# Label-smoothed cross entropy: a ring of three 8000-column buffers, the shorter transfers into buffers of their own, wide tiles worked in two pieces

## The chip, the core and the metric

The kernel runs on one core of a Trainium2 chip. Five engines matter here: PE (TensorE, matrix products), DVE (VectorE, elementwise work and reductions), ACT (ScalarE, functions such as exp and ln), POOL (GpSimd) and SP (SyncE), which computes nothing and here issues the transfers from the chip's main memory into the core's own memory (SBUF). The metric is device time in microseconds (us), from launch to the end of the program.

## The reference

There are 256 rows of 32000 float32 logits and one label to a row. For every row the kernel owes one number:

```python
log_probs = logits - max(logits); log_probs -= log(sum(exp(log_probs)))
smooth_targets[:] = smoothing / num_classes
smooth_targets[i, label] = 1.0 - smoothing + smoothing / num_classes
out = -sum(smooth_targets * log_probs)
```

Since the targets of a row sum to one, the result is log(sum(exp(x))) minus a weighted sum of the logits, in which all have the small weight and the label's logit has the large one besides. So each logit has to be read once (32.77 MB in all), and goes into two sums: one of the logits, one of their exponentials. The kernel takes exp without subtracting the maximum.

## The kernel before, in words

Each of the 128 partitions holds two rows of the input, one after the other, as one line of 64000 columns. The columns are cut into 14 transfers by the table `WIDTHS` (L17): three of 10672, 10672 and 10656 for the first row of each partition, eleven of 8224, 6032, 4480, 3392, 2576, 1984, 1552, 1216, 992, 832 and 720 for the second. A transfer brings one piece of each of the 128 lines; one column of all partitions is 512 bytes.

`load` (L154) issues a transfer on SP (L159). Widths of 1600 and over (`RING_MIN`) go into a ring of three buffers, `xt`, each as wide as the widest tile. That is the first nine transfers, so that the fourth to the ninth wait until the tile three places earlier has been read by DVE and ACT. The five narrower ones go into buffers of their own, `xl`, and wait for no reader. But SP issues in the order of the program, so they stand behind the ninth transfer.

There is one more rule, which the framework adds: transfers of SP and ACT share eight completion semaphores in turn, and a transfer isn't issued before the one that had its semaphore last has landed. The small transfer of the labels, issued by ACT (L103), takes the second of the eight.

Every tile gets two instructions. `sum_logits` (L162) is one pass of DVE that adds the left half of the tile to the right half and accumulates the sum; its elementwise output `jd` is scratch. `sum_exps` (L175) is one pass of ACT that takes exp and accumulates; its elementwise output is scratch too. For tiles wider than 2576 columns (`TURN_MAX`) it goes into the one buffer `ja`, and each such pass waits for the pass before it; the narrower ones take turns in three buffers `jt`. On both engines a short instruction follows that reads the accumulator.

POOL computes the address of each label's logit, fetches these logits with two indirect transfers, and scales them into column 0 of `xsum`. At the end of a row `finish` (L182) takes the logarithm on ACT (L186, L188), turns the two columns of 128 numbers into rows on PE (L190, L194), and combines them on DVE (L195). For the second row the last tiles' sums are added up stepwise (L247 to L255), so that little is left after the last tile; SP then writes the result (L259).

Of the kernel before, what the change touches and what calls it, by code (L numbers as in the profile page):

```python
# [8 lines left out]
FP32 = mybir.dt.float32  # L9
BF16 = mybir.dt.bfloat16  # L10
I32 = mybir.dt.int32
ALU = mybir.AluOpType
AF = mybir.ActivationFunctionType
AX = mybir.AxisListType


WIDTHS = (  # L17
    (10672, 10672, 10656),
    (8224, 6032, 4480, 3392, 2576, 1984, 1552, 1216, 992, 832, 720),
)  # L20

RING_MIN = 1600

TURN_MAX = 2576


def _exp_ln_table(arch: str) -> int | None:
# [30 lines left out]
def kernel(  # L58
# [7 lines left out]
    nc = tc.nc  # L66
    nc.at_finalize(_issue_first_transfers_at_start)
    B, C = logits.shape
    P = nc.NUM_PARTITIONS
# [10 lines left out]
    junk = ctx.enter_context(tc.tile_pool(name="junk", bufs=1))  # L80
    turn = ctx.enter_context(tc.tile_pool(name="turn", bufs=3))
# [7 lines left out]
    if tbl is not None:  # L89
        nc.scalar.add_instruction(  # L90
            mybir.InstLoadActFuncSet(
                name=nc.get_next_instruction_name(),
# [11 lines left out]
        out=lab[:], in_=labels.bitcast(I32).rearrange("(p f) -> p f", p=P)  # L104
    )
    rowoff = small.tile([P, R], I32, name="rowoff", tag="rowoff")
    for r in range(R):
        nc.gpsimd.iota(
            out=rowoff[:, r : r + 1],
# [6 lines left out]
        out=flat_idx[:],  # L116
        in0=rowoff[:],
        in1=lab[:].rearrange("p (r two) -> p r two", two=2)[:, :, 0:1],
        op=ALU.add,
    )  # L120
    gat = small.tile([P, R], FP32, name="gat", tag="gat")
    for r in range(R):
        nc.gpsimd.indirect_dma_start(  # L123
            out=gat[:, r : r + 1],
            out_offset=None,
            in_=logits[:],
# [4 lines left out]
    make_identity(nc, ident[:])  # L131

    label_weight = c_big / c_small
    xsums, esums = [], []
    for r in range(R):
        n = len(WIDTHS[r])
        xsum = small.tile([P, n + 1], FP32, name=f"xsum{r}", tag=f"xsum{r}")  # L140
        esum = small.tile([P, n], FP32, name=f"esum{r}", tag=f"esum{r}")
        nc.gpsimd.tensor_scalar(  # L142
            out=xsum[:, 0:1],
            in0=gat[:, r : r + 1],
            scalar1=label_weight,
            scalar2=None,
            op0=ALU.mult,
        )
        xsums.append(xsum)
        esums.append(esum)  # L150
# [3 lines left out]
    def load(w: int, col: int, name: str):  # L154
        if w >= RING_MIN:
            xt = ring.tile([P, max(WIDTHS[0])], FP32, name="xt", tag="xt")
        else:
            xt = tail.tile([P, w], FP32, name=name, tag=name)
        nc.sync.dma_start(out=xt[:, :w], in_=x[:, col : col + w])  # L159
        return xt  # L160

    def sum_logits(xt, w: int, out: bass.AP):  # L162
        h = w // 2
        jd = junk.tile([P, max(WIDTHS[0]) // 2], FP32, name="jd", tag="jd")
        return nc.vector.scalar_tensor_tensor(  # L165
            out=jd[:, :h],
            in0=xt[:, :h],
            scalar=1.0,
            in1=xt[:, h:w],
            op0=ALU.mult,  # L170
            op1=ALU.add,
            accum_out=out,
        )

    def sum_exps(xt, w: int, out: bass.AP) -> None:  # L175
        if w > TURN_MAX:
            ja = junk.tile([P, max(WIDTHS[0])], BF16, name="ja", tag="ja")
        else:
            ja = turn.tile([P, TURN_MAX], BF16, name="jt", tag="jt")
        nc.scalar.activation(out=ja[:, :w], in_=xt[:, :w], func=AF.Exp, accum_out=out)  # L180

    def finish(r: int, lin: bass.AP, se: bass.AP, se_rest) -> None:  # L182

        lse = small.tile([P, 1], FP32, name=f"lse{r}", tag=f"lse{r}")
        if se_rest is None:
            nc.scalar.activation(out=lse[:], in_=se, func=AF.Ln)  # L186
        else:
            nc.scalar.activation(out=lse[:], in_=se, func=AF.Ln, bias=se_rest)  # L188
        lin_t = psum.tile([1, P], FP32, name=f"lin_t{r}", tag=f"lin_t{r}")
        nc.tensor.transpose(out=lin_t[:], in_=lin, identity=ident[:])  # L190
        lin_row = small.tile([1, P], FP32, name=f"lin_row{r}", tag=f"lin_row{r}")
        nc.vector.tensor_copy(out=lin_row[:], in_=lin_t[:])  # L192
        lse_t = psum.tile([1, P], FP32, name=f"lse_t{r}", tag=f"lse_t{r}")
        nc.tensor.transpose(out=lse_t[:], in_=lse[:], identity=ident[:])  # L194
        nc.vector.scalar_tensor_tensor(  # L195
            out=res[:, :, r : r + 1],
            in0=lin_row[:],
            scalar=-c_small,
            in1=lse_t[:],
            op0=ALU.mult,  # L200
            op1=ALU.add,
        )

    col = 0
    for r in range(R - 1):
        for t, w in enumerate(WIDTHS[r]):
            xt = load(w, col, f"xl{r}_{t}")
            col += w
            sum_logits(xt, w, xsums[r][:, t + 1 : t + 2])
            sum_exps(xt, w, esums[r][:, t : t + 1])  # L210
        both = small.tile([P, 2], FP32, name=f"both{r}", tag=f"both{r}")
        nc.vector.tensor_reduce(  # L212
            out=both[:, 0:1], in_=xsums[r][:], axis=AX.X, op=ALU.add
        )
        nc.vector.tensor_reduce(  # L215
            out=both[:, 1:2], in_=esums[r][:], axis=AX.X, op=ALU.add
        )
        finish(r, both[:, 0:1], both[:, 1:2], None)
# [3 lines left out]
    r = R - 1  # L222
    n = len(WIDTHS[r])
    xsum, esum = xsums[r], esums[r]
    elast = psum.tile([P, 1], FP32, name="elast", tag="elast")
    pairs = [
        small.tile([P, 2], FP32, name=f"pair{i}", tag=f"pair{i}") for i in range(2)
    ]
    done = [
        small.tile([P, 2], FP32, name=f"done{i}", tag=f"done{i}") for i in range(3)  # L230
    ]
    for t, w in enumerate(WIDTHS[r]):
        left = n - 1 - t
        xt = load(w, col, f"xl{r}_{t}")
        col += w
        part = sum_logits(
            xt, w, xsum[:, t + 1 : t + 2] if left > 1 else pairs[1 - left][:, 0:1]
        )
        if left == 0:
            sum_exps(xt, w, elast[:])  # L240
        elif left <= 2:
            sum_exps(xt, w, pairs[2 - left][:, 1:2])
        else:
            sum_exps(xt, w, esum[:, t : t + 1])
        if left == 2:
            with tc.issue_after(part.ins):
                nc.vector.tensor_reduce(  # L247
                    out=done[0][:, 0:1], in_=xsum[:, : t + 2], axis=AX.X, op=ALU.add
                )
                nc.vector.tensor_reduce(  # L250
                    out=done[0][:, 1:2], in_=esum[:, :t], axis=AX.X, op=ALU.add
                )
        elif left < 2:
            i = 1 - left
            nc.vector.tensor_tensor(  # L255
                out=done[i + 1][:], in0=done[i][:], in1=pairs[i][:], op=ALU.add
            )
    finish(r, done[2][:, 0:1], elast[:], done[2][:, 1:2])
    nc.sync.dma_start(  # L259
        out=out.rearrange("(g i) -> g i", g=1), in_=res[:].rearrange("g p r -> g (p r)")  # L260
# [36 lines left out]
```

## Time and profile before

| what | us |
|---|---|
| median of five runs (lowest, highest) | 86.51 (85.44, 86.69) |
| the profiled execution, its time | 85.99 |
| its span, first to last instruction | 83.9 |
| ACT busy, DVE busy, POOL busy in the span | 58.8, 37.6, 14.3 |
| transfer of the logits: share of the 16 DMA engines in the span | 92.3% |

The times of the lines that are shown in the prediction count from the start of the span. About 2.1 us of the execution's own time lie around the span. In a line of the timeline stand the start, the duration, the engine, the line of the kernel, the operation, its output and input with their sizes, and in brackets how long the engine had been idle before and what ended the idle time. An instruction with no brackets began as soon as its engine was free. `xt` and `xl` are the tiles of logits, and 128x2240 in a line of DVE is half of a tile 4480 columns wide.

### The profile page before, as it was taken

What the parts mean: (1) busy time and instruction counts of PE and PEld (TensorE: products, weight loads), DVE (VectorE), ACT (ScalarE), POOL (GpSimd) and SP (SyncE); (2) the same over time, 40 slices, a digit from 0 to 9 for tenths busy, and PEclk for the clock granted to TensorE, in tenths of its full rate; (3) what the DMA queues carried; (4) which work ended last, traced back from release to release, by engine and by line L of the source; (5) the groups of instructions that cost most, each with busy time, mean ns of one, the idle gap of its engine ahead of it and who ended that gap; (6) DMA issues with size and microseconds to landing.
All of it is one profiled execution on the core that took longest, in us unless ns stands there. A gap on an engine that the chain in (4) does not pass through costs nothing.

```text
span 83.9 us, 188 instructions
## 1 busy us (share of the span) xinstructions
PE 1.5 (2%) x4; PEld 0.3 (0%) x4; DVE 37.6 (45%) x38; ACT 58.8 (70%) x31; POOL 14.3 (17%) x13
## 2 busy tenths in 40 slices
PE   0000000000000000000000101000000000000030
PEld 0000000000000000000000000000000000000000
DVE  0000000699000599100599307944909293367760
ACT  5000000699970599980599989999999998799960
POOL 2000000599740599300000000000000000000000
DMA  9889979979979979979899999999999999999300
GB/s 305 346 346 529 428 326 550 427 326 549 427 326 549 427 325 549 427 325 498 361 470 423 439 406 414 437 416 436 419 419 420 389 411 394 409 414 414 148 0 0
DMA packets 2226, 32.77 MB, mean 391 GB/s; under 512 B 433, under 2 KB 434, under 8 KB 1202
## 3 DMA queue, kind: packets, MB, share of 16 engines
q1 hardware_dynamic: 2018, 32.77, 92.3%
q10 hardware_dynamic: 144, 0.00, 0.1%
q0 software_dynamic: 64, 0.00, 0.1%
HBM read 32.77 MB, written 0.00 MB: 391 GB/s over the span
## 4 chain that ended last, share of the span: by engine, by line
DMA 60%; ACT 31%; DVE 3%; SPq 1%; PE 1%; issue 1%; DVEq 0%; ACTq 0%
DMA xt<-in_logits_dram 49%; ACT ja L180 31%; DMA xl<-in_logits_dram 11%; DVE jd L165 2%; SPq L159 1%; PE lse_t L194 0%; PE lin_t L190 0%; DVE done L255 0%; DVE res L195 0%; DVE done L247 0%; DVE done L250 0%; DVEq L255 0%; DVEq L165 0%; ACTq L180 0%
## 5 line engine op out<-in xcount | busy, mean ns | idle before, releaser
L180 ACT ACTIVATE ja<-xt 128x10672 bf16<-128x10672 f32 (+5 forms) x7 | 46.5, 6647 | 20.4 <-DMA xt<-in_logits_dram 20.2
L165 DVE SCALAR_TENSOR_TENSOR jd<-xt 128x5336 f32<-128x5336 f32 (+7 forms) x9 | 32.0, 3553 | 38.1 <-DMA xt<-in_logits_dram 38.1
L115 POOL TENSOR_TENSOR flat_idx<-rowoff,lab 128x2 int32<-128x2 int32 x1 | 5.5, 5475 | 14.4 <-DMA lab<-in_labels_dram 14.4
L142 POOL TENSOR_SCALAR xsum<-gat 128x1 f32<-128x1 f32 x2 | 6.0, 2985 | 4.3 <-DMA gat<-in_logits_dram,flat_idx 4.2
L180 ACT ACTIVATE jt<-xl 128x1552 bf16<-128x1552 f32 (+4 forms) x5 | 5.4, 1083 | 0.0
L180 ACT ACTIVATE jt<-xt 128x2576 bf16<-128x2576 f32 (+1 forms) x2 | 4.2, 2104 | 0.8 <-DMA xt<-in_logits_dram 0.8
L165 DVE SCALAR_TENSOR_TENSOR jd<-xl 128x776 f32<-128x776 f32 (+4 forms) x5 | 3.6, 713 | 1.6 <-DMA xl<-in_logits_dram 1.6
L123 POOL DMA_INDIRECT gat<-in_logits_dram,flat_idx x2 | 2.1, 1053 | 0.5 <-issue 0.3
L90 ACT ACT_TABLE_LOAD x1 | 1.3, 1283 | 0.9 <-PEq L278 0.9
L180 ACT ACTIVATION_READ_ACCUMULATOR ja<-xt 128x1 f32 x7 | 1.3, 186 | 0.0
L215 DVE TENSOR_REDUCE both<-esum 128x1 f32<-128x3 f32 x1 | 0.2, 155 | 2.5 <-ACT ja L180 2.5
L190 PE MATMUL lin_t<-ident,both 128*1 128x128 f32 x1 | 0.4, 374 | 46.8 <-DVE both L212 46.8
L192 DVE COPY lin_row<-lin_t 1x128 f32<-1x128 f32 x2 | 0.6, 279 | 0.9 <-PE lin_t L190 0.9
L195 DVE SCALAR_TENSOR_TENSOR res<-lin_row,lse_t 1x128 f32<-1x128 f32 x2 | 0.6, 276 | 0.8 <-PE lse_t L194 0.7
L190 PE MATMUL lin_t<-ident,done 128*1 128x128 f32 x1 | 0.4, 373 | 30.0 <-DVE done L255 30.0
L180 ACT ACTIVATION_READ_ACCUMULATOR jt<-xl 128x1 f32 x5 | 0.9, 179 | 0.0
L194 PE MATMUL lse_t<-ident,lse 128*1 128x128 f32 x2 | 0.7, 374 | 3.3 <-ACT lse L186 3.2
L165 DVE DVE_READ_ACCUMULATOR jd<-xt 128x1 f32 x9 | 0.7, 82 | 0.0
L255 DVE TENSOR_TENSOR done<-done,pair 128x2 f32<-128x2 f32 x2 | 0.3, 160 | 0.2
L165 DVE DVE_READ_ACCUMULATOR jd<-xl 128x1 f32 x5 | 0.4, 82 | 0.0
L180 ACT ACTIVATION_READ_ACCUMULATOR jt<-xt 128x1 f32 x2 | 0.4, 187 | 0.0
L186 ACT ACTIVATE lse<-both 128x1 f32<-128x1 f32 x1 | 0.2, 203 | 0.2 <-DVE both L215 0.2
(14 smaller groups left out, 2.1 us busy)
## 6 DMA issues: line engine op xcount, KB each, us to landing
xt<-in_logits_dram SPq DMA_DIRECT2D x2, 5336.0 KB, 21.3
xt<-in_logits_dram SPq DMA_DIRECT2D x1, 5328.0 KB, 39.4
xt<-in_logits_dram SPq DMA_DIRECT2D x1, 4112.0 KB, 25.8
xt<-in_logits_dram SPq DMA_DIRECT2D x1, 3016.0 KB, 20.2
xt<-in_logits_dram SPq DMA_DIRECT2D x1, 2240.0 KB, 13.0
xt<-in_logits_dram SPq DMA_DIRECT2D x1, 1696.0 KB
xt<-in_logits_dram SPq DMA_DIRECT2D x1, 1288.0 KB, 7.4
xt<-in_logits_dram SPq DMA_DIRECT2D x1, 992.0 KB, 6.3
```

The source lines that it names most:

```text
L90: nc.scalar.add_instruction(mybir.InstLoadActFuncSet(name=nc.get_next_instruction_name(), act_func_set_id=tbl, ins=[], outs=[],))
L115: nc.gpsimd.tensor_tensor(out=flat_idx[:], in0=rowoff[:], in1=lab[:].rearrange("p (r two) -> p r two", two=2)[:, :, 0:1], op=ALU.add,)
L123: nc.gpsimd.indirect_dma_start(out=gat[:, r : r + 1], out_offset=None, in_=logits[:], in_offset=bass.IndirectOffsetOnAxis(ap=flat_idx[:, r ...
L142: nc.gpsimd.tensor_scalar(out=xsum[:, 0:1], in0=gat[:, r : r + 1], scalar1=label_weight, scalar2=None, op0=ALU.mult,)
L159: nc.sync.dma_start(out=xt[:, :w], in_=x[:, col : col + w])
L165: return nc.vector.scalar_tensor_tensor(out=jd[:, :h], in0=xt[:, :h], scalar=1.0, in1=xt[:, h:w], op0=ALU.mult, op1=ALU.add, accum_out=out,)
L180: nc.scalar.activation(out=ja[:, :w], in_=xt[:, :w], func=AF.Exp, accum_out=out)
L190: nc.tensor.transpose(out=lin_t[:], in_=lin, identity=ident[:])
L192: nc.vector.tensor_copy(out=lin_row[:], in_=lin_t[:])
L194: nc.tensor.transpose(out=lse_t[:], in_=lse[:], identity=ident[:])
L195: nc.vector.scalar_tensor_tensor(out=res[:, :, r : r + 1], in0=lin_row[:], scalar=-c_small, in1=lse_t[:], op0=ALU.mult, op1=ALU.add,)
L255: nc.vector.tensor_tensor(out=done[i + 1][:], in0=done[i][:], in1=pairs[i][:], op=ALU.add)
```

## The change

The widths become 8000 four times for the first row and 8000, 6272, 4736, 3648, 2688, 2048, 1536, 1216, 1024 and 832 for the second, all multiples of 64, and again 14 transfers in all. The ring's three buffers are 8000 columns wide and hold only widths of 6000 and over, which are the first six transfers. The other eight have buffers of their own. A tile is worked in as many equal pieces as are needed for none to exceed 4032 columns (`PIECE`): the 8000, the 6272 and the 4736 become two pieces each, the others stay whole. So ACT and DVE have 21 passes each where they had 14. The scratch of DVE and ACT shrinks to the size of a piece, and all of ACT's scratch now takes turns in three buffers.

```diff
 WIDTHS = (
-    (10672, 10672, 10656),
-    (8224, 6032, 4480, 3392, 2576, 1984, 1552, 1216, 992, 832, 720),
+    (8000, 8000, 8000, 8000),
+    (8000, 6272, 4736, 3648, 2688, 2048, 1536, 1216, 1024, 832),
 )
-RING_MIN = 1600
-TURN_MAX = 2576
+RING_MIN = 6000
+PIECE = 4032
...
+    pieces = [[-(-w // PIECE) for w in ws] for ws in WIDTHS]
...
-        jd = junk.tile([P, max(WIDTHS[0]) // 2], FP32, name="jd", tag="jd")
+        jd = junk.tile([P, PIECE // 2], FP32, name="jd", tag="jd")
...
-    def sum_exps(xt, w: int, out: bass.AP) -> None:
-        if w > TURN_MAX:
-            ja = junk.tile([P, max(WIDTHS[0])], BF16, name="ja", tag="ja")
-        else:
-            ja = turn.tile([P, TURN_MAX], BF16, name="jt", tag="jt")
-        nc.scalar.activation(out=ja[:, :w], in_=xt[:, :w], func=AF.Exp, accum_out=out)
+    def sum_exps(xp, w: int, out: bass.AP) -> None:
+        ja = turn.tile([P, PIECE], BF16, name="ja", tag="ja")
+        nc.scalar.activation(out=ja[:, :w], in_=xp, func=AF.Exp, accum_out=out)
...
-            sum_logits(xt, w, xsums[r][:, t + 1 : t + 2])
-            sum_exps(xt, w, esums[r][:, t : t + 1])
+            k = pieces[r][t]
+            for i in range(k):
+                xp = xt[:, i * (w // k) : (i + 1) * (w // k)]
+                sum_logits(xp, w // k, xsums[r][:, at + 1 : at + 2])
+                sum_exps(xp, w // k, esums[r][:, at : at + 1])
+                at += 1
```

The loop over the second row is changed in the same way: a loop over the pieces, with a running index `at` for the columns of the partial sums.

More of the change, by code (lines that the diff above doesn't have):

```diff
@@ L131 @@
     make_identity(nc, ident[:])
+    pieces = [[-(-w // PIECE) for w in ws] for ws in WIDTHS]
+    assert all(w % (2 * k) == 0 for ws, ks in zip(WIDTHS, pieces) for w, k in zip(ws, ks))
     label_weight = c_big / c_small
@@ L138 @@
     for r in range(R):
-        n = len(WIDTHS[r])
+        n = sum(pieces[r])
         xsum = small.tile([P, n + 1], FP32, name=f"xsum{r}", tag=f"xsum{r}")
@@ L160, in load, with sum_logits @@
         return xt
-    def sum_logits(xt, w: int, out: bass.AP):
+    def sum_logits(xp, w: int, out: bass.AP):
         h = w // 2
-        jd = junk.tile([P, max(WIDTHS[0]) // 2], FP32, name="jd", tag="jd")
+        jd = junk.tile([P, PIECE // 2], FP32, name="jd", tag="jd")
         return nc.vector.scalar_tensor_tensor(
             out=jd[:, :h],
-            in0=xt[:, :h],
+            in0=xp[:, :h],
             scalar=1.0,
-            in1=xt[:, h:w],
+            in1=xp[:, h:w],
             op0=ALU.mult,
@@ L205 @@
     for r in range(R - 1):
+        at = 0
         for t, w in enumerate(WIDTHS[r]):
@@ L231 @@
     ]
+    at = 0
     for t, w in enumerate(WIDTHS[r]):
@@ L235 @@
         col += w
[L236 to L244, printed above, removed]
+        k = pieces[r][t]
+        assert k == 1 or left > 2
+        for i in range(k):
+            xp = xt[:, i * (w // k) : (i + 1) * (w // k)]
+            part = sum_logits(
+                xp,
+                w // k,
+                xsum[:, at + 1 : at + 2] if left > 1 else pairs[1 - left][:, 0:1],
+            )
+            if left == 0:
+                to = elast[:]
+            elif left <= 2:
+                to = pairs[2 - left][:, 1:2]
+            else:
+                to = esum[:, at : at + 1]
+            sum_exps(xp, w // k, to)
+            at += 1
         if left == 2:
@@ L247 @@
                 nc.vector.tensor_reduce(
-                    out=done[0][:, 0:1], in_=xsum[:, : t + 2], axis=AX.X, op=ALU.add
+                    out=done[0][:, 0:1], in_=xsum[:, : at + 1], axis=AX.X, op=ALU.add
                 )
                 nc.vector.tensor_reduce(
-                    out=done[0][:, 1:2], in_=esum[:, :t], axis=AX.X, op=ALU.add
+                    out=done[0][:, 1:2], in_=esum[:, : at - 1], axis=AX.X, op=ALU.add
                 )
```

## The prediction, made before the changed kernel was run

> **What bounds the kernel now.** I looked first at the page's slices and its chain of work that ended last:
>
> ```profile
> DMA  9889979979979979979899999999999999999300
> GB/s 305 346 346 529 428 326 550 427 326 549 427 326 549 427 325 549 427 325 498 361 470 423 439 406 414 437 416 436 419 419 420 389 411 394 409 414 414 148 0 0
> ...
> DMA 60%; ACT 31%; DVE 3%; SPq 1%; PE 1%; issue 1%; DVEq 0%; ACTq 0%
> ```
>
> The DMA engines are busy from start to slice 37, and the chain is mostly transfers. So the question is whether they move bytes evenly. The busy times by stretch (start:end, length, busy PE, PEld, DVE, ACT, POOL, clock, DMA share, GB/s) say not quite:
>
> ```profile
> 52.00:65.00 13.00, 0.00 (x0) 0.00 (x0) 8.76 (x5) 12.94 (x5) 0.00 (x0) 1.00 1.00 428
> 65.00:72.00 7.00, 0.00 (x0) 0.00 (x0) 3.94 (x6) 6.75 (x5) 0.00 (x0) 1.00 0.97 397
> 72.00:78.00 6.00, 0.00 (x0) 0.00 (x0) 3.01 (x8) 5.47 (x8) 0.00 (x0) 1.00 1.00 412
> ```
>
> Then the timeline of DVE, which stands idle before most tiles, so that its starts give the landings:
>
> ```profile
> 15.43 5.72 DVE L165 SCALAR_TENSOR_TENSOR jd<-xt 128x5336 f32<-128x5336 f32 x1 [15.43 <-DMA xt<-in_logits_dram]
> ...
> 40.80 5.71 DVE L165 SCALAR_TENSOR_TENSOR jd<-xt 128x5328 f32<-128x5328 f32 x1 [6.82 <-DMA xt<-in_logits_dram]
> ...
> 57.70 3.30 DVE L165 SCALAR_TENSOR_TENSOR jd<-xt 128x3016 f32<-128x3016 f32 x1 [2.21 <-DMA xt<-in_logits_dram]
> ...
> 63.04 2.49 DVE L165 SCALAR_TENSOR_TENSOR jd<-xt 128x2240 f32<-128x2240 f32 x1 [2.03 <-DMA xt<-in_logits_dram]
> ...
> 67.10 1.93 DVE L165 SCALAR_TENSOR_TENSOR jd<-xt 128x1696 f32<-128x1696 f32 x1 [1.56 <-DMA xt<-in_logits_dram]
> ...
> 70.53 1.50 DVE L165 SCALAR_TENSOR_TENSOR jd<-xt 128x1288 f32<-128x1288 f32 x1 [1.50 <-DMA xt<-in_logits_dram]
> ...
> 73.50 1.19 DVE L165 SCALAR_TENSOR_TENSOR jd<-xt 128x992 f32<-128x992 f32 x1 [1.47 <-DMA xt<-in_logits_dram]
> ...
> 75.37 0.97 DVE L165 SCALAR_TENSOR_TENSOR jd<-xl 128x776 f32<-128x776 f32 x1 [0.67 <-DMA xl<-in_logits_dram]
> ```
>
> From the first landing (15.43, 10672 columns) to the seventh (67.10, 54128 columns) 43456 columns took 51.67 us: **1.189 ns a column**. The eighth (2576 columns) took 3.36 us where that rate gives 3.06, the ninth (1984) 2.97 where it gives 2.36: 0.30 and 0.61 late, **0.91 us together** (ACT's starts at 70.46 and 73.43 taken). The narrower ones are back near the rate (1552 in 1.9 us, 1.22 ns). What is special about these two? SP's timeline:
>
> ```profile
> 67.49 3.31 SPq L159 DMA_DIRECT2D xl<-in_logits_dram  x5
> ```
>
> The ninth was issued at 67.11, just before these five, when ACT had freed its buffer; from 63.05 to 67.11 only one transfer stood in the queue behind the one that was landing, where from 25 us to 50 whole tiles did. Last ACT, which comes after the landings:
>
> ```profile
> 57.48 0.19 ACT L180 ACTIVATION_READ_ACCUMULATOR ja<-xt 128x1 f32 x1
> 57.70 5.23 ACT L180 ACTIVATE ja<-xt 128x6032 bf16<-128x6032 f32 x1
> ...
> 70.46 2.35 ACT L180 ACTIVATE jt<-xt 128x2576 bf16<-128x2576 f32 x1 [0.22 <-DMA xt<-in_logits_dram]
> ...
> 73.43 1.86 ACT L180 ACTIVATE jt<-xt 128x1984 bf16<-128x1984 f32 x1 [0.53 <-DMA xt<-in_logits_dram]
> ...
> 75.30 1.50 ACT L180 ACTIVATE jt<-xl 128x1552 bf16<-128x1552 f32 x1
> ...
> 78.06 1.03 ACT L180 ACTIVATE jt<-xl 128x992 bf16<-128x992 f32 x1
> ...
> 79.09 0.88 ACT L180 ACTIVATE jt<-xl 128x832 bf16<-128x832 f32 x1
> ...
> 80.86 0.26 ACT L188 ACTIVATE lse<-elast,done 128x1 f32<-128x1 f32 x1
> ```
>
> After 73.43 it hardly waits; the last pass (720, from 79.98) ends at 80.77, and the logarithm and the output follow. So the late ninth landing is what the end pays for, through ACT.
>
> **The change part by part.**
>
> *Passes.* ACT's rows give 0.8333 ns a column and 0.203 us fixed (8224: 7.057; 2576: 2.351; 992: 1.030). Seven more passes add 1.4 us to ACT, beside transfers as long as the tile's landing interval is longer. A pass into `jt` starts when the duration of the one before is over, its accumulator read half done (78.06 + 1.03 = 79.09); into `ja` 0.12 later (50.52 + 7.06 = 57.58, start 57.70), though a landing fell there too. All are of the first kind now, so I charge durations alone; the other end, 0.12 a pass, is kept as a rival. DVE's seven more cost 0.17 us and a read of 0.08 each, hidden: an 8000 tile takes it 4.6 us, and tiles come every 9.5. If that cover went, ACT's 7.1 for the same tile would still be last.
>
> *Ring and queue.* The first tile lands 2672 columns earlier: 15.43 - 3.18 = 12.25. ACT has read it at 19.33, when the fourth transfer is issued; transfers two and three keep the engines busy until 31.28, 12 us of cover. The sixth goes out at 38.35, and behind it, with nothing to wait for, the seventh to eleventh. The twelfth to fourteenth share semaphores with the fourth to sixth, and go out as these land, the last at 57.8: 20 us before it is needed. SP has nothing else to issue until the result. So the two thin landings have a full queue: **0.91 at most, 0 at least**. I take all of it, since the rows before and after keep the rate with a queue behind them.
>
> *Labels, POOL.* The label transfer landed with the first tile (POOL started at 15.73) and will move with it; POOL's sums were done at 34.3 and are wanted after 46, so nothing.
>
> *The end.* Landings at 1.189 ns: sixth (46272 columns) 57.76, then 63.39, 67.73, 70.92, 73.36, 75.18, 76.63, 77.85, last 78.84. ACT takes the sixth at 57.76 and from there never waits: 2 x 2.816 (3136 columns each), 2 x 2.176, 3.243, 2.443, 1.910, 1.483, 1.217, 1.056 and, by the row above, 0.884 come to 22.22. It ends at **79.98** instead of 80.77. The last tile's pass is 0.1 longer (832 for 720), which is counted there. DVE's last pass (0.59) is over before. The sum: 85.99 - 0.79 = **85.20**. ACT can't get earlier than this unless the sixth tile lands earlier.
>
> The 85.99 lies between the runs at 85.4 to 85.7 and those at 86.5 to 86.7, whose median is 86.51. From that median it would be 85.7; between both I say **85.5**.
>
> *Widths in multiples of 64.* The transfer that began at column 32000, such a multiple, had 1.173 ns a column (40.79 to 50.44, 8224 columns); the three after it, off such multiples, 1.19 to 1.20, but so had the third, also off, 1.178, and the ninth, on one, was slowest. Bounds: 0, and 0.012 on all 64000 columns, 0.77 us. I take 0. The Trainium skill ("DMA: Bandwidth & Descriptors", How a descriptor splits into AXI transactions) says that a read starting off a 256-byte boundary fetches the bytes below it as well. Ten of the 14 old transfers start so, eight rows on each engine, some 160 bytes each; at 27 GB/s an engine, an estimate from that page, it is 0.5 us, and the sum would be 84.7. The rows neither settle nor exclude it.
>
> **The rivals.**
>
> *Nothing gained* (0.21): the two late landings come of SP issuing six transfers in a row, or of their size, not of a thin queue. For it: 412 GB/s also after 72, with the queue full. The loss stays, ACT ends at 80.82: **86.05**.
>
> *Faster rows by alignment* (0.16): 1.177 ns throughout; the sixth lands at 57.2, ACT ends at 79.42: **84.65**.
>
> *A long queue is slow* (0.11), the other side: the stretches at 397 and 412 GB/s are also those in which up to six transfers stood in the queue. If the queue itself costs the engines their rate, it will do so from 40 us on, for 32000 columns. At 412 (1.243 ns) ACT ends at 81.47, 0.70 later; at 397 (1.290), 82.95, 2.18 later. The middle is **87.4**. It decides as soon as the late rate falls below 420 GB/s (1.219 ns). Against it: the first 40 us also have up to two whole tiles queued, and no loss.
>
> *ACT's passes don't overlap* (0.07): 0.12 on each of the 12 from the sixth tile on, ACT ends at 81.3: **86.5**. A change that doesn't do what it says is in the first rival; only the last three transfers are held, harmlessly.
>
> **How the numbers follow.** The forecast has 0.45. Range 84.6 to 86.9: it takes in alignment below, nothing gained and slow passes above, and leaves out most of the long queue (0.08) and the edges. One per cent, 0.86 us, is about what a measurement of this kernel can tell from no change. The forecast's 0.79 lies just inside, some 0.17 of its 0.45 beyond; with alignment 0.33 for faster. Slower over 1% is most of the long queue with a little of ACT's, 0.10. The rest, 0.57, is the same.
>
> **What will show it.** Right: landings of the 2688 and 2048 tiles 2.4 to 2.6 apart, ACT with no idle time from the sixth tile on, GB/s near 428 until 72. Alignment: 435 in most stretches, landings of 8000 in 9.42. Nothing gained: a dip near 40 us or again in the small tiles, and ACT waiting there. Long queue: under 420 from 40 us. I am wrong at the root if landings slip further for the deeply queued tiles, or if ACT waits at the end although the data is there.

## The result, and the profile after

The changed kernel takes **85.38 us** (median of 52 runs, 85.17 to 85.89) where the kernel before takes 85.84 (median of 94 runs, 85.14 to 87.44). The ratio is 0.9959, with a 95% interval of 0.9947 to 0.9972. That ratio leaves out runs more than 1.5% above the fastest, which are 20 of the 94 and none of the 52; the medians of all runs differ by 0.46 us. The forecast was 85.5, with 0.79 us gained in the sum; so the direction was right and the gain a little over half of what the sum said.

One thing stands in the runs and in no single profile: the *fastest* runs of the two kernels are alike (85.14 and 85.17). What differs is the spread, 2.3 us before and 0.7 after. The change removes a loss that the kernel before has in some executions and not in others. The equal times also hide a trade. The fastest runs of the kernel before that are on record with their spans (85.10 to 85.17) have spans of 83.0 to 83.2 us and 1.9 to 2.1 around them; the fastest of the changed kernel (85.17) has 83.4 and 1.8.

The profiled execution took 85.43 us, with a span of 83.6. The chain of work that ended last, from the page of the changed kernel, shares of the span:

```profile
DMA 84%; ACT 9%; DVE 2%; issue 1%; PE 0%; SPq 0%; DVEq 0%; ACTq 0%
```

Most of ACT's 31% of before has gone into transfers. The busy times by stretch of the changed kernel (columns as in the prediction):

```profile
52.00:65.00 13.00, 0.00 (x0) 0.00 (x0) 7.89 (x11) 12.70 (x9) 0.00 (x0) 1.00 0.99 424
65.00:72.00 7.00, 0.00 (x0) 0.00 (x0) 4.29 (x5) 7.00 (x7) 0.00 (x0) 1.00 1.01 425
72.00:78.00 6.00, 0.00 (x0) 0.00 (x0) 3.85 (x10) 6.00 (x7) 0.00 (x0) 1.00 1.01 408
```

The dip of before between 65 and 72 us (397 GB/s) is gone: 425. The last six microseconds are no faster than they were (408, 412 before). Its timeline of DVE gives the landings, and that of ACT what follows:

```profile
71.10 1.56 DVE L169 SCALAR_TENSOR_TENSOR jd<-xl 128x1344 f32<-128x1344 f32 x1 [1.18 <-DMA xl<-in_logits_dram]
...
73.59 1.23 DVE L169 SCALAR_TENSOR_TENSOR jd<-xl 128x1024 f32<-128x1024 f32 x1 [0.92 <-DMA xl<-in_logits_dram]
...
75.49 0.96 DVE L169 SCALAR_TENSOR_TENSOR jd<-xl 128x768 f32<-128x768 f32 x1 [0.66 <-DMA xl<-in_logits_dram]
...
79.00 0.16 DVE L270 TENSOR_TENSOR done<-done,pair 128x2 f32<-128x2 f32 x1
79.45 0.59 DVE L169 SCALAR_TENSOR_TENSOR jd<-xl 128x416 f32<-128x416 f32 x1 [0.29 <-DMA xl<-in_logits_dram]
```

```profile
57.83 2.82 ACT L181 ACTIVATE ja<-xt 128x3136 bf16<-128x3136 f32 x1 [0.30 <-DMA xt<-in_logits_dram]
...
71.09 2.44 ACT L181 ACTIVATE ja<-xl 128x2688 bf16<-128x2688 f32 x1
...
79.31 0.88 ACT L181 ACTIVATE ja<-xl 128x832 bf16<-128x832 f32 x1
...
80.41 0.26 ACT L189 ACTIVATE lse<-elast,done 128x1 f32<-128x1 f32 x1 [0.17 <-DVE done L270]
```

The 2688 and 2048 tiles land 3.24 and 2.49 us after the one before, where 1.189 ns a column gives 3.20 and 2.44: the two late landings don't occur. Once ACT has begun the sixth tile (57.83), it has no bracket until the logarithm, which waits for DVE now. And DVE shows something odd: it starts the last tile 0.14 us *after* ACT, although ACT already reads the same tile and DVE has been idle for 0.29.

### The profile page after: what moved, and what is told of

It is laid out like the page before. It is cut to its first block, busy times and chain, and to the rows that moved or that the text cites. A ratio compares the mean times of both kernels' runs of the same rounds, so it can differ in the third digit from the quotient of the medians.

```text
span 83.6 us, 214 instructions
## 1 busy us (share of the span) xinstructions
PE 1.5 (2%) x4; PEld 0.3 (0%) x4; DVE 38.9 (47%) x52; ACT 59.9 (72%) x45; POOL 7.2 (9%) x13
## 4 chain that ended last, share of the span: by engine, by line
DMA 84%; ACT 9%; DVE 2%; issue 1%; PE 0%; SPq 0%; DVEq 0%; ACTq 0%
DMA xt<-in_logits_dram 59%; DMA xl<-in_logits_dram 26%; ACT ja L181 9%; DVE jd L169 1%; PE lin_t L191 0%; SPq L163 0%; DVE lin_row L193 0%; DVE res L196 0%; DVE done L270 0%; DVEq L196 0%; DVEq L270 0%; ACTq L181 0%
## 5 line engine op out<-in xcount | busy, mean ns | idle before, releaser
L181 ACT ACTIVATE ja<-xt 128x4000 bf16<-128x4000 f32 (+1 forms) x12 | 40.9, 3409 | 19.5 <-DMA xt<-in_logits_dram 19.5
L169 DVE SCALAR_TENSOR_TENSOR jd<-xt 128x2000 f32<-128x2000 f32 (+1 forms) x12 | 26.1, 2176 | 31.5 <-DMA xt<-in_logits_dram 31.3
L181 ACT ACTIVATE ja<-xl 128x2368 bf16<-128x2368 f32 (+7 forms) x9 | 16.6, 1840 | 0.0
L169 DVE SCALAR_TENSOR_TENSOR jd<-xl 128x1184 f32<-128x1184 f32 (+7 forms) x9 | 10.7, 1184 | 7.3 <-DMA xl<-in_logits_dram 7.1
L123 POOL DMA_INDIRECT gat<-in_logits_dram,flat_idx x2 | 3.9, 1938 | 0.5 <-issue 0.3
L115 POOL TENSOR_TENSOR flat_idx<-rowoff,lab 128x2 int32<-128x2 int32 x1 | 2.0, 1990 | 11.2 <-DMA lab<-in_labels_dram 11.2
L181 ACT ACTIVATION_READ_ACCUMULATOR ja<-xt 128x1 f32 x12 | 2.2, 186 | 0.0
L181 ACT ACTIVATION_READ_ACCUMULATOR ja<-xl 128x1 f32 x9 | 1.6, 182 | 0.0
L146 POOL TENSOR_SCALAR xsum<-gat 128x1 f32<-128x1 f32 x2 | 0.6, 276 | 6.8 <-DMA gat<-in_logits_dram,flat_idx 6.8
```

Source lines behind the costliest of these rows:

```text
L115: nc.gpsimd.tensor_tensor(out=flat_idx[:], in0=rowoff[:], in1=lab[:].rearrange("p (r two) -> p r two", two=2)[:, :, 0:1], op=ALU.add,)
L123: nc.gpsimd.indirect_dma_start(out=gat[:, r : r + 1], out_offset=None, in_=logits[:], in_offset=bass.IndirectOffsetOnAxis(ap=flat_idx[:, r ...
L146: nc.gpsimd.tensor_scalar(out=xsum[:, 0:1], in0=gat[:, r : r + 1], scalar1=label_weight, scalar2=None, op0=ALU.mult,)
L169: return nc.vector.scalar_tensor_tensor(out=jd[:, :h], in0=xp[:, :h], scalar=1.0, in1=xp[:, h:w], op0=ALU.mult, op1=ALU.add, accum_out=out,)
L181: nc.scalar.activation(out=ja[:, :w], in_=xp, func=AF.Exp, accum_out=out)
```

## The experiments

Each ratio is to runs of the kernel before on the same chip; their medians were 85.59 to 85.68 us. The edits are to the changed kernel, unless another run is named. The queue of transfers is called thin when only one stands behind the one that is landing.

### Is it the early issue, the alignment, or the passes?

**late_issue.** Only the ring's lower bound goes back.

```diff
-RING_MIN = 6000
+RING_MIN = 1600
```

> The changed kernel with only the ring's lower bound put back to 1600: the 4736, 3648, 2688 and 2048 tiles go into the ring again and wait for a buffer, and the four narrowest stand behind them on SP. Thin queue: the 2688 and 2048 landings come 0.3 to 0.9 us late again, ACT waits before them, and the median goes back to that of the kernel before (about 85.9), with its wide spread from run to run. If the gain came of the alignment or of the passes instead: the median stays at 85.4 and the landings keep to 1.19 to 1.22 ns a column.

Measured: median 85.69, single runs from 85.28 to 86.78 (12 runs); ratio to the kernel before 1.0027 (0.9993 to 1.0062). The gain is gone and the wide spread is back. The profiled execution was the fastest of the twelve, at 85.28, and shows no late landing: its 2688 and 2048 tiles landed at 70.95 and 73.42. So the lateness comes and goes from one execution to the next, and a profile can miss it.

**off_boundary.** All transfers but the first of each row begin off a multiple of 64 columns.

```diff
-    (8000, 8000, 8000, 8000),
-    (8000, 6272, 4736, 3648, 2688, 2048, 1536, 1216, 1024, 832),
+    (7984, 8000, 8000, 8016),
+    (7984, 6272, 4736, 3648, 2688, 2048, 1536, 1216, 1024, 848),
```

> The changed kernel with the first width of each row 16 columns (64 bytes) narrower and the last 16 wider, so that all transfers but the first of each row begin off a multiple of 64 columns. Alignment counts: up to 0.5 us later, landings of the 8000 tiles at 9.55 us or more instead of 9.5. It doesn't count: 85.4, but for some 0.02 us for a last tile of 848.

Measured: median 85.23 (85.15 to 85.44), ratio 0.9963 (0.9933 to 0.9992), so not later than the changed kernel. Its tiles of some 8000 columns landed at 12.09, 21.67, 31.25, 40.72 and 50.08; those of the changed kernel at 12.22, 21.86, 31.42, 40.90 and 50.32, no closer together. Alignment to 64 columns is worth nothing here that these runs can see. The price that the Trainium skill ("DMA: Bandwidth & Descriptors", How a descriptor splits into AXI transactions) led me to estimate at 0.5 us doesn't show (85.23 against 85.38); the measurement decides.

**one_scratch.** One scratch buffer of ACT for three.

```diff
-    turn = ctx.enter_context(tc.tile_pool(name="turn", bufs=3))
+    turn = ctx.enter_context(tc.tile_pool(name="turn", bufs=1))
```

> The changed kernel with one scratch buffer for ACT instead of three that take turns, so that each pass waits for the one before to be done. If the passes overlap thanks to the three buffers: 0.12 us on each of the 12 passes from the sixth tile on, less what ACT waited for landings there, so the end of ACT 1.0 to 1.3 later and the time 86.2 to 86.6. If the overlap isn't due to the buffers: 85.4.

Measured: median 86.22 (86.16 to 86.35), ratio 1.0082 (1.0042 to 1.0122), about 0.8 above the changed kernel. ACT's timeline of this run:

```profile
68.25 3.24 ACT L181 ACTIVATE ja<-xl 128x3648 bf16<-128x3648 f32 x1
...
71.61 2.44 ACT L181 ACTIVATE ja<-xl 128x2688 bf16<-128x2688 f32 x1
...
74.18 1.91 ACT L181 ACTIVATE ja<-xl 128x2048 bf16<-128x2048 f32 x1
```

From start to start 3.36 and 2.57 us, where the durations are 3.24 and 2.44: 0.12 to 0.13 more a pass, with no wait for data. So the overlap comes of the buffers taking turns, and with it the seven added passes stay cheap.

### Is it the thin queue, or the issues in a row?

In the kernel before, the late landings fall together with SP issuing six transfers within 3.2 us. Three runs take the two apart.

**all_in_ring.** Every transfer waits for a buffer; SP never issues two in a row after the start.

```diff
-RING_MIN = 6000
+RING_MIN = 0
```

> The changed kernel with every tile in the ring: each transfer is issued when the tile three places before has been read, so that there is no stretch in which SP issues several in a row, and never more than two or three are queued. Thin queue: most landings from the 2688 tile on come late, each by some 0.3 us, and the time is 86.5 or more. Burst of issues: nothing lands late, and the time is 85.4, that of the changed kernel.

Measured: median 87.91 (87.30 to 89.42, six runs), ratio 1.0277 (1.0223 to 1.0331). ACT's timeline:

```profile
73.44 1.91 ACT L181 ACTIVATE ja<-xt 128x2048 bf16<-128x2048 f32 x1
...
75.66 1.48 ACT L181 ACTIVATE ja<-xt 128x1536 bf16<-128x1536 f32 x1 [0.21 <-DMA xt<-in_logits_dram]
...
78.25 1.22 ACT L181 ACTIVATE ja<-xt 128x1216 bf16<-128x1216 f32 x1 [1.01 <-DMA xt<-in_logits_dram]
...
80.05 1.06 ACT L181 ACTIVATE ja<-xt 128x1024 bf16<-128x1024 f32 x1 [0.49 <-DMA xt<-in_logits_dram]
```

Lateness without any burst, but not where I had put it: the 2688 and 2048 tiles were in time in this execution, and the narrower ones starve outright. The 1536 tile was issued at 71.1 and landed 4.5 us later; for 2.3 of them the tile ahead was still landing (until 73.45). From landing to landing the 1536, 1216, 1024 and 832 tiles took 2.22, 2.59, 1.73 and 1.27 us, where their bytes take 1.83, 1.45, 1.22 and 0.99 at the usual rate: 0.3 to 1.1 late each. And the rate itself falls, to 257 to 321 GB/s in each stretch of 2 us from 72 to 80, where the changed kernel moved 408 from 72 to 78. So two transfers at a time, each issued 4.0 to 4.6 us before its landing, don't keep the engines busy here.

**late_burst.** The queue stays deep, but the last four issues come late and in a row: they use the 4736 tile's memory again (issues from 68.1 on).

```diff
-        xt = load(w, col, f"xl{r}_{t}")
+        if left == 3:
+            at_col, again = col, tail.tile([P, 4736], FP32, name="xl1_2", tag="xl1_2")
+        if left <= 3:
+            xt = again[:, col - at_col : col - at_col + w]
+            nc.sync.dma_start(out=xt, in_=x[:, col : col + w])
+        else:
+            xt = load(w, col, f"xl{r}_{t}")
```

> The changed kernel, in which the four narrowest tiles (1536 to 832) share the memory of the 4736 tile and are therefore issued only when that has been read, in a row from about 67.8 us; the 3648, 2688 and 2048 tiles stay issued early, so that the queue is deep all the time. If SP issuing several transfers in a row slows the engines just then: the 2688 and 2048 tiles land up to 0.9 late in some executions, the median is 85.6 or more and the single runs spread over a microsecond as in the kernel before. If only a thin queue does: 85.4, spread of 0.3 as in the changed kernel.

Measured: median 85.49 (85.32 to 85.85), ratio 0.9982 (0.9948 to 1.0015). The median lies between the two expected ones; the spread of 0.5 us is like that of the changed kernel, where the kernel before has 1.4 on this chip.

**late_no_burst.** The opposite: late_issue with its last four transfers made one.

```diff
-        xt = load(w, col, f"xl{r}_{t}")
+        if left == 3:
+            tail_at, tail_w = col, sum(WIDTHS[r][t:])
+            whole = tail.tile([P, tail_w], FP32, name="xlast", tag="xlast")
+            nc.sync.dma_start(out=whole[:], in_=x[:, col : col + tail_w])
+        if left <= 3:
+            xt = whole[:, col - tail_at : col - tail_at + w]
+        else:
+            xt = load(w, col, f"xl{r}_{t}")
```

> The kernel of the run late_issue (the 4736 to 2048 tiles in the ring again), with its last four transfers made one, so that there are only two issues in a row at 67.8. All four last tiles wait for the one landing, which makes the time some 3.4 us longer, about 88.8; what is read is the spread, since any lateness moves the last landing. Thin queue: single runs spread over a microsecond or more. Burst of issues: they stay within 0.3 us.

Measured: median 89.33, single runs from 88.77 to 89.64 (six runs), ratio 1.0411 (1.0355 to 1.0468). They spread over 0.87 us, a little under the microsecond expected of a thin queue and far over the 0.3 expected of a burst. Here the profile caught a late one. ACT's timeline of late_burst, then of late_no_burst:

```profile
71.28 2.44 ACT L181 ACTIVATE ja<-xl 128x2688 bf16<-128x2688 f32 x1
...
73.77 1.91 ACT L181 ACTIVATE ja<-xl 128x2048 bf16<-128x2048 f32 x1
```

```profile
71.04 2.44 ACT L181 ACTIVATE ja<-xt 128x2688 bf16<-128x2688 f32 x1
...
74.39 1.91 ACT L181 ACTIVATE ja<-xt 128x2048 bf16<-128x2048 f32 x1 [0.82 <-DMA xt<-in_logits_dram]
```

With the burst and a deep queue the 2048 tile is 2.49 us behind the 2688, as in the changed kernel; with a thin queue and no burst it is 3.35 behind, 0.9 late. So the thin queue is the cause, and the burst is not. How a thin queue delays a landing, and what varies from one execution to the next so that it sometimes does no harm, stays open.

### Are the new widths needed for it?

**old_widths_early** and **old_widths_pieces.** The widths of before, worked in pieces, which frees memory; the two runs differ only in whether the 2576 and 1984 tiles are in the ring: the bound is 2600 in the first, as shown, and 1600 in the second.

```diff
 WIDTHS = (
-    (8000, 8000, 8000, 8000),
-    (8000, 6272, 4736, 3648, 2688, 2048, 1536, 1216, 1024, 832),
+    (10672, 10672, 10656),
+    (8224, 6032, 4480, 3392, 2576, 1984, 1552, 1216, 992, 832, 720),
 )
-RING_MIN = 6000
-PIECE = 4032
+RING_MIN = 2600
+PIECE = 5336
...
-    turn = ctx.enter_context(tc.tile_pool(name="turn", bufs=3))
+    turn = ctx.enter_context(tc.tile_pool(name="turn", bufs=2))
```

> The widths of the kernel before, with tiles worked in pieces of at most 5336 columns and ACT's scratch taking turns in two buffers (which makes room), and the 2576 and 1984 tiles in buffers of their own, so that they are issued with the five narrower ones behind the 3392 tile at about 58 us. Thin queue: the queue is deep from there on, no landing is late, and the time is 85.2 to 85.5 with the narrow spread of the changed kernel; the new widths are not needed for it. If it is the new widths (even taper, multiples of 64) that count: no better than the kernel before, 85.6 to 85.9.

> The same, but with the 2576 and 1984 tiles in the ring as in the kernel before, issued late: pieces and scratch alone. Thin queue: single runs up to 86.5 again and a median of 85.6 to 86.0, a median 0.2 to 0.5 above the run with the early issue. If pieces and scratch are what helps: 85.2 to 85.5, like that run.

Measured: 84.96 (84.85 to 85.23), ratio 0.9914 (0.9884 to 0.9944), with the early issue; 86.25 (85.52 to 87.12), ratio 1.0029 (0.9986 to 1.0072), without. Both ran on one chip, where the kernel before has 85.62. ACT's timeline with the early issue, then without:

```profile
70.52 2.35 ACT L181 ACTIVATE ja<-xl 128x2576 bf16<-128x2576 f32 x1
...
72.88 1.86 ACT L181 ACTIVATE ja<-xl 128x1984 bf16<-128x1984 f32 x1
```

```profile
71.11 2.35 ACT L181 ACTIVATE ja<-xt 128x2576 bf16<-128x2576 f32 x1 [0.75 <-DMA xt<-in_logits_dram]
...
73.74 1.86 ACT L181 ACTIVATE ja<-xt 128x1984 bf16<-128x1984 f32 x1 [0.19 <-DMA xt<-in_logits_dram]
```

Moving two transfers out of the ring is worth 1.3 us here, and the kernel with the old widths beats both kernels of this study. So the new widths are not what helps, and pieces with two scratch buffers gain nothing without the early issue; their median is even 0.6 above the kernel before, for which no run gives the reason. That the new widths cost something is likely (the medians are 0.4 apart, on different chips; the last tile is 832 wide for 720), but was not measured by itself.

### Where did the rest of the forecast gain go?

**merged_tail.** The last six transfers made one.

```diff
-        if w >= RING_MIN:
+        if w >= RING_MIN and name != "xlast":
...
-        xt = load(w, col, f"xl{r}_{t}")
+        if left == 5:
+            tail_at, tail_w = col, sum(WIDTHS[r][t:])
+            whole = load(tail_w, col, "xlast")
+        if left <= 5:
+            xt = whole[:, col - tail_at : col - tail_at + w]
+        else:
+            xt = load(w, col, f"xl{r}_{t}")
```

> The changed kernel with the last six transfers (2688 to 832, 9344 columns) made one; their passes all wait for it, so the time will be some 8 us longer, and only the landing is read. If each transfer has a small price of its own (about 0.05 us, which the forecast left out), the one lands at 78.9, some 0.3 before the last of the six (79.2 to 79.3). If the engines finish unevenly at the end whatever the number of transfers, it lands at 79.2 as well.

Measured: 93.39 us (one run). The landing, in ACT's timeline of this run:

```profile
78.90 2.44 ACT L181 ACTIVATE ja<-xlast 128x2688 bf16<-128x2688 f32 x1 [7.72 <-DMA xlast<-in_logits_dram]
```

78.90, where 1.189 ns a column gives 78.84. In the changed kernel the last of the six lands between 79.2 (the trace's own mark, at the end of a transfer of 21.42 us from 57.77) and 79.31, when ACT starts on it. Up to the tile before the two executions keep step (ACT starts on the 3648 tile at 67.84 and 67.85). So each of the five further transfers costs 0.06 to 0.08 us, by one execution of each kernel. The forecast had left that out.

**dve_whole.** DVE takes each tile in one pass again; the loop over the second row is changed in the same way.

```diff
-        jd = junk.tile([P, PIECE // 2], FP32, name="jd", tag="jd")
+        jd = junk.tile([P, max(WIDTHS[0]) // 2], FP32, name="jd", tag="jd")
...
                 xp = xt[:, i * (w // k) : (i + 1) * (w // k)]
-                sum_logits(xp, w // k, xsums[r][:, at + 1 : at + 2])
+                if i == 0:
+                    sum_logits(xt, w, xsums[r][:, t + 1 : t + 2])
...
```

> The changed kernel with DVE taking each tile in one pass (14 instead of 21), ACT in pieces as before. In the changed kernel DVE starts the last tile's pass 0.14 us after ACT and 0.29 after its own instruction before, though ACT already has the data. If that gap is a stall in the supply of DVE's instructions at a certain place of its program, it moves or goes with the seven passes (and their reads), and the logarithm starts 0.1 to 0.2 earlier: 85.2. If the gap belongs to the last transfer's landing, it stays: 85.4.

Measured: 85.55 (85.39 to 85.65), ratio 0.9981 (0.9947 to 1.0015). DVE's timeline:

```profile
79.05 0.16 DVE L272 TENSOR_TENSOR done<-done,pair 128x2 f32<-128x2 f32 x1
79.24 0.59 DVE L169 SCALAR_TENSOR_TENSOR jd<-xl 128x416 f32<-128x416 f32 x1
```

The gap is gone, and DVE starts before ACT (79.36): it had not been the landing. But the time did not fall. The span is 83.5, and 2.15 us lie around it where the changed kernel has 1.83.

**early_whole_6032.** The best kernel so far (old_widths_early), with the 6032 tile in one pass.

```diff
-PIECE = 5336
+PIECE = 6032
```

> The widths of the kernel before with the early issue (the run old_widths_early), pieces of up to 6032 columns, so that the 6032 tile is one pass of ACT. If ACT's passes from that tile on set the end: 0.1 to 0.2 less than 84.96. If the last landing does: 84.9 to 85.0, the same.

Measured: 85.75 (85.52 to 86.03), ratio 1.0020 (0.9991 to 1.0049): a pass less, and 0.8 slower than old_widths_early. Neither expectation held. The end of its timeline:

```profile
80.27 0.26 ACT L189 ACTIVATE lse<-elast,done 128x1 f32<-128x1 f32 x1
...
80.58 0.28 DVE L193 COPY lin_row<-lin_t 1x128 f32<-1x128 f32 x1 [0.47 <-PE lin_t L191]
81.38 0.28 DVE L196 SCALAR_TENSOR_TENSOR res<-lin_row,lse_t 1x128 f32<-1x128 f32 x1 [0.52 <-PE lse_t L195]
```

The logarithm starts earlier than in the changed kernel (80.27), but PE's product (from 80.58, 0.37 long) is done at 80.95 and DVE's last instruction comes at 81.38; the chain calls 0.41 of it "issue", time in which the engine waited for nothing that the profile shows. Again 2.13 us lie around the span. This gap and that of the changed kernel stand before the same place of DVE's program. I had counted its 71st instruction, in the listing of the program; in the records of both traces, waits on semaphores included, it is the 64th of DVE. The kernels with some 2.1 us around the span (the one before, dve_whole, merged_tail and this one) have an engine, DVE or ACT, whose program ends just short of that place: 60 recorded instructions or fewer, where all others have 62 or more on both engines.

**early_whole_padded.** The same kernel with useless instructions ahead of the first tile.

```diff
+    zero = small.tile([1, 1], FP32, name="zero", tag="zero")
+    nc.vector.memset(zero[:], 0.0)
+    pad_v = small.tile([1, 23], FP32, name="pad_v", tag="pad_v")
+    for i in range(23):
+        nc.vector.memset(pad_v[:, i : i + 1], 0.0)
+    pad_a = small.tile([1, 48], FP32, name="pad_a", tag="pad_a")
+    for i in range(48):
+        nc.scalar.activation(out=pad_a[:, i : i + 1], in_=zero[:], func=AF.Copy)
```

> The run early_whole_6032 with 24 one-element writes of DVE and 48 one-element copies of ACT put ahead of the first tile, while both engines wait for it. They compute nothing that is used. In early_whole_6032 DVE stood still for 0.41 us before its last instruction, in the changed kernel for 0.29 before the last tile's pass, each at about the 71st instruction of DVE's program (semaphore waits counted), and where DVE or ACT has fewer instructions than that, some 2.1 us lie around the span instead of 1.8. If an engine stalls for its next block of instructions at that place, the extra instructions move the place to where the engines wait for transfers anyway: no gap at the end, 1.8 around the span, and 84.8 to 85.1 instead of 85.75. If the two gaps have other causes: 85.7 or more, since there is only more to do.

Measured: 85.25 (85.09 to 85.47), ratio 0.9959 (0.9934 to 0.9984). Seventy-two more instructions make the kernel 0.5 us *faster*. The end of its timeline:

```profile
81.13 0.28 DVE L205 SCALAR_TENSOR_TENSOR res<-lin_row,lse_t 1x128 f32<-1x128 f32 x1
```

No gap before the last instruction, and 1.75 us around the span. The time missed the expected 84.8 to 85.1 by 0.15; the pass saved does not show. (ACT waited 0.24 us for the 832 tile in this execution, and not in the one of early_whole_6032.) DVE's 64th recorded instruction is its pass on the 1984 tile now, and the stall has gone there:

```profile
72.64 1.85 ACT L190 ACTIVATE ja<-xl 128x1984 bf16<-128x1984 f32 x1
...
73.06 1.19 DVE L178 SCALAR_TENSOR_TENSOR jd<-xl 128x992 f32<-128x992 f32 x1 [1.25 <-DMA xl<-in_logits_dram]
```

ACT reads the tile from 72.64 on, so its data was there, and DVE begins 0.42 us later. Nothing waits for DVE at that place.

The page of a run also lists a DMA queue for instructions (q14). In the changed kernel it moves one packet, between 80.0 and 80.2 us, in early_whole_6032 one falls between 82.0 and 82.2, and in early_whole_padded one between 44 and 45 and one between 76.3 and 76.6. So the packet near a gap starts after the gap is over (79.45, 81.38 and 73.06), and DVE did not wait for it.

## Why the prediction was right, and by how much it was off

- *A late landing of two tiles, caused by a thin queue*: right. late_no_burst has the lateness without the burst, late_burst the burst without the lateness, and two transfers moved out of the ring gain 1.3 us with the old widths as well.
- *"I take all of it"*, 0.91 us: **this is the mis-sized term**. The 0.91 was that of one execution. Over 94 runs the kernel before lies between 85.14 and 87.44. Its fastest runs, with spans of 83.0 to 83.2 where the profiled one has 83.9, have hardly any of the loss, and the median of all runs is 0.7 above the best. A term read from one profile had to be set beside the spread of the runs shown, 85.44 to 86.69, which was already wider than anything in the chain explained.
- *85.5*: near the measured 85.38, but partly by luck. It is the middle between 85.20, from the profiled execution, and 85.7, from a median of five runs (86.51) that 94 runs put at 85.84. From 85.84 the sum gives 85.05, 0.33 too low. By an estimate from these numbers, some 0.2 of that is the loss taken at 0.91 where a typical run has 0.7; the rest is what the next three items leave over (0.21 and 0.17 us lost, 0.26 won).
- *Landings at 1.189 ns a column to the end*: right to the fourth tile of the second row (57.76 forecast, 57.83; 63.39, 63.48; 67.73, 67.85), then short: 73.36 against 73.58, 75.18 against 75.49, 78.84 against 79.2 to 79.3. The term left out is 0.06 to 0.08 us a transfer (merged_tail).
- *ACT never waits from the sixth tile on and ends at 79.98*: it never waited noticeably, and ended at 79.31 + 0.88 = 80.19, with the landings. Charging durations alone was right: one_scratch shows 0.12 to 0.13 a pass if the scratch doesn't take turns. (The rival names 12 passes from the sixth tile on; there are 11, and its 81.3 is worked out with 11.)
- *"DVE's last pass is over before"*: wrong. DVE began the last tile at 79.45, its sum was ready at 80.33, and the logarithm waited 0.17 for it. The stall of 0.29 before that pass was on the path, because the seven DVE passes that I had called hidden brought a fixed place of DVE's program there (dve_whole; the last section has more). In exchange 1.83 us instead of 2.09 lie around the span. From profile to profile: span 0.3 shorter, 0.26 less around it, 0.56 together, where the sum said 0.79.
- *Alignment at nothing*: right (off_boundary). *A long queue is slow*: refuted, with 425 GB/s between 65 and 72 us under the deepest queue. *The order on SP and the shared semaphores*: as forecast, the last two transfers at 50.3 and 57.8.

## What to carry to other kernels

When a stream of transfers tapers, give the narrow ones memory of their own and issue them so early that more than one always stands behind the one that is landing. A slot of a ring that comes free only one or two narrow tiles before it is needed leaves the queue thin, and the loss comes and goes from run to run. So read the spread of the runs beside the profile, and never size a term by one execution alone. And at the end of a short kernel, a gap that no wait explains may belong to a fixed place of the engine's program, which a few instructions more or fewer move.

## What the runs showed of the hardware that was not expected

DVE stands still at a fixed place of its own program, whatever the instruction there: between its 63rd and its 64th, counted in the records of the trace with waits on semaphores included. The start of the second comes 0.45 us after the start of the first in the changed kernel (79.00 to 79.45), late_issue, off_boundary and late_burst, 0.47 in all_in_ring, and 0.48 in early_whole_6032 (80.90 to 81.38) and early_whole_padded (72.58 to 73.06), though the 63rd itself takes 0.02 to 0.16. Where DVE waits at that place anyway, the stall doesn't show. In old_widths_early the 64th waits 0.47 us for PE, with or without it. In one_scratch the 63rd had waited 0.37 for ACT, and the 64th follows 0.18 after it.

Moving the place by adding useless instructions took 0.5 us off the time (85.75 to 85.25). Part of that lies outside the span: where DVE or ACT has 60 recorded instructions or fewer, 2.0 to 2.1 us lie around it, on the mean of a kernel's runs, and 1.8 where both have 62 or more.

What holds the engine there was not seen. A fixed place by count suggests the supply of the program's next block of instructions, but the one packet that the instruction queue moves near it starts after the gap. So that remains a guess.
